# Matmul with RMSNorm: the right half of row blocks 2 and 3 as seven Strassen products, streamed with B

## The chip, the cores and the metric

The kernel runs on one core of a Trainium2 chip. The metric is the device time of one execution in microseconds (us); the median of three runs of the kernel before is 224.25 us (224.13 to 224.69).

## The reference

```python
# a: 2048x2048, b: 2048x2048, gamma: 2048, all fp32; eps = 1e-5
x = np.matmul(a, b)
rms = np.sqrt(np.mean(x ** 2, axis=-1, keepdims=True) + eps)
return gamma * x / rms
```

So each row of the product is divided by its own root mean square and multiplied by gamma. A row can be written out only when all of its 2048 columns are known.

## The kernel before

**Tiles.** A is cut into 16 row blocks of 128 rows, B into eight pieces of 256 rows (`KP`, each piece two steps `kt` of 128), and each of these into a left and a right half of 1024 columns (`j` = 0, 1; one half has two chunks of `CH` = 512 columns). B is cast to bf16 while it is loaded and stays on the chip. A matmul has 128 rows of A, 128 of k and 512 columns, and writes one PSUM bank. There are eight banks: seven in the pool `ps_a` (tiles `acc`), handed out in the order in which they come free, and one in `ps_t` (`tbank`).

**Head.** Row blocks 0 to 3 (`HB` = 4) are computed the plain way while B arrives. In the left half (loop over `kp`, `groups1`) TensorE transposes each arriving piece of A (`transpose_head`, L160), VectorE copies it into `head_at`, and seven chunks collect in seven banks; the eighth (row block 3, chunk 1) goes through `tbank` in parts that VectorE adds up (`stream_in_parts`, L379). In the right half (`groups2`) it is the same with seven chunks in seven banks and no transposes of the head; the eighth chunk follows at the end by itself (L459 to L466).

**Body.** Row blocks 4 to 15 are taken in pairs, the groups `g` = 2 to 7. Such a group has 256 rows; with a half of B it makes a 2x2 block product, computed by Strassen's scheme in seven products of 8 matmuls instead of eight. `a_sums` (L238) builds the sums of A's quarters (`s_sum`, 128x1024 16-bit each), `b_sums` (L249) three sums of B's quarters per piece into `sums`, and `b_sum_7`, `b_sum_6` and `b_sums_in_place` put two more in place of B's own quarters, which may happen only when no plain matmul needs them any more. `group_half` (L483) gives the order of products, 2, 5, 1, 4, 3, 7, 6, with these lines at its start:

```python
t = x22
at_hook(0)
product(g, j, 2, p2)
c = spare if (g, j) == (G0, 0) else t
nc.scalar.copy(out=c, in_=p2)
at_hook(1)
product(g, j, 5, p5)
nc.vector.tensor_tensor(out=t, in0=p5, in1=c, op=ALU.add)
```

Product 4 then accumulates onto the bank of product 2, product 3 onto that of product 5 (`start=False`), so each has to wait until the earlier contents have been read.

**Rows of A for the body.** `load_block` brings 128 rows (1 MB) through GpSimd's DMA queue into one of two buffers of `a_pool`. `row_norm` (L204, ScalarE: two squares over 1024 elements with a sum, one root), `row_factor` (L215, four short steps on VectorE) and `row_apply` (L226, VectorE for blocks 4 and 5, ScalarE after that) scale the rows to fp16. Blocks 4 and 5 are transposed by TensorE (`transpose_half`, L174, copied out by VectorE), the others by DMA (`transpose_dma`, on SP's queue).

**End of a row.** `square` (L287, ScalarE) sums the squares of 512 columns; `take_rms` (L313) adds them up on VectorE and takes the root on ScalarE; `finish` (L334) multiplies by gamma and 1/rms on VectorE, half a row at a time, and issues the output DMA from SP. The eight half-row buffers `x_slot` are used again: row block 4's left half takes the place of row block 0's left one, row block 5's left half (where the first group's `x21`, `x22` lie) that of row block 0's right one.

**What sets the order.** The schedule is written by hand (`manual_schedule`): every engine works strictly in the order in which the program calls it, and waits are put in where data or a buffer demands it. The `hooks` of `hooks_of` (L535) place side work between the products. GpSimd's queue of loads is written out as a list, `later` (L357): pieces 0 to 4 of B's right half, row block 4, B 5, B 6, row block 5, B 7; then gamma, blocks 6 and 7 (these wait until blocks 4 and 5 have left `a_pool`), and later blocks after a `wait_for`.

Of the kernel before, what the change touches and what calls it, by code (L numbers as in the profile page):

```python
# [17 lines left out]
def kernel(  # L18
# [32 lines left out]
    stat_pool = ctx.enter_context(tc.tile_pool(name="stat_pool", bufs=8))  # L51
# [25 lines left out]
    spare = head_at.rearrange("p t r m -> p (t r m)")[:, K:2 * K].bitcast(FP32)[:, 0:CH]  # L77

    def a16_slot(mb):

        if mb < HB + 2:
            return x_slot[HB + 1 + 2 * (mb % 2)].bitcast(FP16)
        flat = head_at.rearrange("p t r m -> p (t r m)").bitcast(FP16)
        return flat[:, (2 + mb % 2) * K:(3 + mb % 2) * K]
# [27 lines left out]

    def load_block(mb):
        a32[mb] = a_pool.tile([P, K], FP32, name="a32")
        nc.gpsimd.dma_start(out=a32[mb], in_=a[mb * P:(mb + 1) * P, :])
# [8 lines left out]
    identity_f = consts.tile([P, P], FP32, name="identity_f")  # L124
# [4 lines left out]
    nc.vector.memset(warm, 0.0)  # L129
    identity = consts.tile([P, P], BF16, name="identity")  # L130
# [43 lines left out]
    def transpose_half(mb, g):  # L174
        bank = ps_t.tile([P, CH], FP32, name="tbank")
# [7 lines left out]
        nc.vector.tensor_copy(out=at(mb)[:, g * 8:(g + 1) * 8, :], in_=view)  # L183
# [8 lines left out]
    def new_msq(mb):  # L192
        msq[mb] = stat_pool.tile([P, NCH + 1], FP32, name="msq")
        n_sq[mb] = 0

    for mb in range(HB):
        new_msq(mb)
        nc.gpsimd.memset(msq[mb][:, NCH:], float(eps))
# [27 lines left out]
    def row_apply(mb):  # L226
        a16[mb] = a16_slot(mb)
        if mb < HB + 2:
            nc.vector.tensor_scalar_mul(out=a16[mb], in0=a32.pop(mb), scalar1=factor.pop(mb))
# [5 lines left out]
    def quarter(g, r, c):  # L235
        return at(2 * g + r)[:, c::2, :]

    def a_sums(g, which):  # L238
# [3 lines left out]
        for s in which:  # L242
            x, y, op = terms[s]
            nc.vector.tensor_tensor(out=s_sum[s], in0=x, in1=y, op=op)  # L244
# [11 lines left out]
    def b_sum_7(j, kp):  # L256

        b21, b22 = (b_quarter(j, kp, 1, c) for c in range(2))
        nc.vector.tensor_tensor(out=b21, in0=b21, in1=b22, op=ALU.add)

    def b_sum_6(j, kp):

        b11, b12 = (b_quarter(j, kp, 0, c) for c in range(2))
        nc.vector.tensor_tensor(out=b12, in0=b12, in1=b11, op=ALU.add)

# [6 lines left out]
    def product(g, j, m, bank, start=True):  # L272
        for kp in range(KP):
            lhsT = {3: quarter(g, 0, 0), 4: quarter(g, 1, 1)}[m] if m in (3, 4) else s_sum[m]
            rhs = {1: lambda: sums[j][:, 0, kp, :], 2: lambda: b_quarter(j, kp, 0, 0),
                   3: lambda: sums[j][:, 1, kp, :], 4: lambda: sums[j][:, 2, kp, :],
                   5: lambda: b_quarter(j, kp, 1, 1), 6: lambda: b_quarter(j, kp, 0, 1),
                   7: lambda: b_quarter(j, kp, 1, 0)}[m]()
            nc.tensor.matmul(bank, lhsT[:, kp, :], rhs,  # L279
                             start=(start and kp == 0), stop=(kp == KP - 1),  # L280
                             skip_group_check=not start)
# [5 lines left out]
    def square(mb, src):  # L287
# [3 lines left out]
        nc.scalar.activation(out=sq[:, 0:CH], in_=src, func=ACTF.Square,  # L291
                             scale=inv_sqrt_n, accum_out=msq[mb][:, c:c + 1])
# [60 lines left out]
    def new_bank():  # L353
        return ps_a.tile([P, CH], FP32, name="acc")

    later = ([("b", kp) for kp in range(5)]
             + [("a", HB), ("b", 5), ("b", 6), ("a", HB + 1), ("b", 7)])  # L357

    def load_later(n):
        for _ in range(min(n, len(later))):  # L360
            kind, which = later.pop(0)
            load_b(1, which) if kind == "b" else load_block(which)
# [31 lines left out]

    groups1 = [(r, c) for r in range(HB) for c in range(2)][:-1]
    last1 = (HB - 1, 1)
    banks = {}
    for r in range(HB):
        x_tile(r, 0)
    transpose_first()  # L400
    for kp in range(KP):
# [4 lines left out]
        before = [lambda: transpose_head(kp + 1)] if kp + 1 < KP else []  # L406
        stream(groups1, kp, before, len(groups1) + 5 if kp == 0 else None)
# [3 lines left out]
        if kp > 0:  # L411
            b_sums(0, kp - 1)
    load_later(2)
    b_sums(0, KP - 1)


    def prepare(mb):
        row_norm(mb)
        row_factor(mb)
        row_apply(mb)  # L420

    def b_sums_2(kp):
        b_sums_in_place(0, kp)
        b_sums(1, kp)
        if kp + 1 < KP:
            b_sum_7(1, kp)

    r3 = HB - 1
    squares = groups1 + [last1]
    groups2 = [(r, c) for r in range(HB) for c in (2, 3)][:-1]  # L430
    for kp in range(KP):
        load_later(1)
        before = [lambda: transpose_half(HB, 0)] if kp == 6 else []
        if kp == 7:
            before = [lambda: transpose_half(HB, 1)]
        stream(groups2, kp, before)
        square(squares[kp][0], x_chunk(*squares[kp]))
        if kp == 4:
            prepare(HB)
        if kp == 6:  # L440

            prepare(HB + 1)
        elif kp == KP - 1:
            b_sums_in_place(0, kp - 1)
        else:
            b_sums_2(kp)
# [3 lines left out]


    def squares2(r):
        for c in (2, 3):
            square(r, x_chunk(r, c))

    evict(groups2[0:2], ())
    squares2(0)
    evict(groups2[2:-1], ())
    bank = new_bank()  # L459
    for kt in range(KT):  # L460
        if kt in (0, 6):
# [275 lines left out]
```

## Time and profile before

| what | value |
|---|---|
| median of the runs | 224.25 us |
| span of the profiled execution, first to last instruction | 222.6 us |
| what lies between the two | 1.65 us |
| TensorE matmul busy | 211.1 us, 95% |
| VectorE busy | 161.8 us, 73% |
| ScalarE busy | 129.1 us, 58% |
| GpSimd busy | 24.5 us, 11% |
| mean granted TensorE clock | 0.993 |
| DMA moved | 47.13 MB, 212 GB/s |

The profile shows one execution. The profiled execution's own device time is not given beside its span, so the median of the runs stands for it. Times are from the start of the span; L279 is line 279 of the kernel, PEld is TensorE's loading of weights. A line of a group or of the timeline has the source line, the engine, the operation, output<-inputs and the shape. Duration is that of one instruction alone; where two follow each other on one engine, the second may start some 0.1 us before the first one's end.

### The profile page before, as it was taken

The page shows a single profiled execution, that of the slowest core. Times are in us where ns is not written, and L with a number is a line of the kernel's source. Part 1 is how long each engine was busy: PE and PEld are TensorE (multiplying, and loading weights), DVE is VectorE, ACT ScalarE, POOL GpSimd, SP SyncE. Part 2 cuts the span into 40 slices and gives each one's busy share as a digit, 9 for nine tenths or more (in the row PEclk, how much of TensorE's full clock was granted, in tenths as well). Part 3 has the DMA queues.
Part 4 walks back from the last instruction along what each step waited for, and adds up shares of the span by engine and source line. Part 5 has one row for each costly group of instructions (what it writes and reads, how often), then busy time and mean ns, then how long its engine had stood idle before and what let it go on. Part 6 is the DMA issues. An engine that isn't in the chain of part 4 may idle for free.

```text
span 222.6 us, 3026 instructions
## 1 busy us (share of the span) xinstructions
PE 211.1 (95%) x1043; PEld 98.6 (44%) x1043; DVE 161.8 (73%) x324; ACT 129.1 (58%) x272; POOL 24.5 (11%) x49
## 2 busy tenths in 40 slices
PE   7899999999999999999999999999999999999950
PEld 2445444444454444444444444444444444444430
DVE  2427557983999989978949298837994589587692
ACT  3110002807698895799646985699478954334570
POOL 7534232300000001000100002000200000000000
PEclk9999999999999999999999999999999999999997
DMA  6999999999973499818889259945994794044045
GB/s 184 223 202 209 203 208 211 212 303 259 327 280 159 188 272 292 310 72 226 276 228 400 58 174 222 366 151 143 246 368 168 97 282 189 0 188 193 0 190 188
DMA packets 36176, 47.13 MB, mean 212 GB/s; under 512 B 21952, under 2 KB 26048, under 8 KB 34496
## 3 DMA queue, kind: packets, MB, share of 16 engines
q0 software_dynamic: 9648, 23.33, 41.6%
q1 hardware_dynamic: 26080, 22.29, 33.0%
q10 hardware_dynamic: 432, 1.31, 2.0%
q8 instruction: 8, 0.13, 0.2%
q14 instruction: 8, 0.07, 0.1%
HBM read 34.60 MB, written 16.78 MB: 231 GB/s over the span
## 4 chain that ended last, share of the span: by engine, by line
PE 83%; DMA 8%; DVE 2%; POOL 2%; issue 1%; ACT 1%; DVEq 0%; ACTq 0%; POOLq 0%
PE acc L279 63%; PE acc L350 18%; DMA b<-in_b_dram 8%; POOL early L106 1%; DVE x L617 1%; POOL b L100 1%; DVE x L620 1%; PE tbank L179 1%; PE tbank L382 1%; PE tbank L165 1%; ACT sq L291 0%; DVEq L732 0%; ACT sq L682 0%; DVE x L690 0%; DVE r L322 0%
## 5 line engine op out<-in xcount | busy, mean ns | idle before, releaser
L279 PE MATMUL acc<-b,s 128*128 128x512 bf16 x376 | 83.3, 379 | 0.0
L279 PEld LDWEIGHTS <-s 128*128 128x128 f16 x472 | 46.2, 98 | 55.7 <-DVE s L244 0.2
L350 PE MATMUL acc<-b,head_at 128*128 128x512 bf16 x240 | 55.1, 379 | 0.6 <-DMA b<-in_b_dram 0.4
L291 ACT ACTIVATE sq<-x 128x512 bf16<-128x512 f32 x62 | 39.1, 631 | 10.9 <-DVE x L520 5.1
L340 DVE SCALAR_TENSOR_TENSOR x<-x,r,gamma_sb 128x1024 f32<-128x1024 f32 x28 | 34.7, 1282 | 0.8
L209 ACT ACTIVATE sq<-a 128x1024 bf16<-128x1024 f32 x24 | 25.4, 1057 | 16.8 <-DMA a<-in_a_dram 16.4
L350 PEld LDWEIGHTS <-head_at 128*128 128x128 bf16 x240 | 22.9, 98 | 26.7 <-issue 1.1
L393 ACT COPY x<-acc 128x512 f32<-128x512 f32 x11 | 5.9, 591 | 25.1 <-PE acc L350 25.1
L231 ACT ACTIVATE head_at<-a,s 128x2048 f16<-128x2048 f32 x10 | 19.9, 1990 | 0.0
L279 PEld LDWEIGHTS <-at_even 128*128 128x128 f16 x96 | 9.4, 98 | 11.5 <-issue 0.4
L279 PEld LDWEIGHTS <-head_at 128*128 128x128 f16 x96 | 9.4, 98 | 11.3
L100 POOL DMA_DIRECT2D b<-in_b_dram x15 | 10.6, 708 | 16.0 <-DMA b<-in_b_dram 13.2
L217 DVE TENSOR_SCALAR s<-norm 128x1 f32<-128x1 f32 x12 | 1.8, 150 | 14.3 <-ACT norm L212 14.2
L244 DVE TENSOR_TENSOR s<-at_even 128x1024 f16<-128x1024 f16 x15 | 9.7, 684 | 2.8 <-DMA at_even<-head_at 2.8
L291 ACT ACTIVATION_READ_ACCUMULATOR sq<-x 128x1 f32 x62 | 11.7, 188 | 0.0
L279 PE MATMUL acc<-t_left,s 128*128 128x512 bf16 x48 | 11.3, 379 | 0.0
L279 PE MATMUL acc<-early,s 128*128 128x512 bf16 x48 | 11.3, 379 | 0.0
L279 PE MATMUL acc<-early,at_even 128*128 128x512 bf16 x48 | 11.0, 379 | 0.0
L279 PE MATMUL acc<-t_left,at_even 128*128 128x512 bf16 x48 | 10.9, 379 | 0.0
L509 ACT COPY x<-acc 128x512 f32<-128x512 f32 x10 | 5.7, 575 | 8.9 <-PE acc L279 8.9
L279 PE MATMUL acc<-t_left,head_at 128*128 128x512 bf16 x48 | 10.8, 379 | 0.0
L279 PE MATMUL acc<-early,head_at 128*128 128x512 bf16 x48 | 10.8, 379 | 0.0
(86 smaller groups left out, 205.8 us busy)
## 6 DMA issues: line engine op xcount, KB each, us to landing
out_dram<-x SPq DMA_DIRECT2D x30, 512.0 KB, 3.1
a<-in_a_dram POOLq DMA_DIRECT2D x12, 1024.0 KB, 8.5
b<-in_b_dram POOLq DMA_DIRECT2D x15, 512.0 KB, 17.1
early<-in_a_dram POOLq DMA_DIRECT2D x7, 256.0 KB, 14.8
early<-in_b_dram ACTq DMA_DIRECT2D x2, 512.0 KB, 5.9
gamma_sb<-in_gamma_dram POOLq DMA_DIRECT2D x1, 1024.0 KB, 19.9
out_dram<-x SPq DMA_DIRECT2D x3, 256.0 KB, 3.5
early<-in_a_dram SPq DMA_DIRECT2D x1, 512.0 KB, 5.7
```

The costliest lines, as they stand in the source:

```text
L100: nc.gpsimd.dma_start(out=raw[j][kp], in_=b[kp * W2:(kp + 1) * W2, j * HALF:(j + 1) * HALF].rearrange("(t p) n -> p t n", p=P))
L106: nc.gpsimd.dma_start(out=ah(kp), in_=a[0:HB * P, kp * W2:(kp + 1) * W2].rearrange("(r p) k -> p r k", p=P))
L165: nc.tensor.matmul(view[:, t, r, :], ah(kp)[:, r, t * P:(t + 1) * P], identity, is_transpose=True, start=(t == 0 and r == 0), stop=(t == 1 ...
L209: nc.scalar.activation(out=junk, in_=a32[mb][:, h * HALF:(h + 1) * HALF], func=ACTF.Square, scale=2.0 ** -8, accum_out=n2[:, h:h + 1])
L231: nc.scalar.activation(out=a16[mb], in_=a32.pop(mb), func=ACTF.Copy, scale=factor.pop(mb))
L244: nc.vector.tensor_tensor(out=s_sum[s], in0=x, in1=y, op=op)
L279: nc.tensor.matmul(bank, lhsT[:, kp, :], rhs, start=(start and kp == 0), stop=(kp == KP - 1), skip_group_check=not start)
L291: nc.scalar.activation(out=sq[:, 0:CH], in_=src, func=ACTF.Square, scale=inv_sqrt_n, accum_out=msq[mb][:, c:c + 1])
L340: nc.vector.scalar_tensor_tensor(out=x, in0=x, scalar=r, in1=gamma_sb[:, h * HALF:(h + 1) * HALF], op0=ALU.mult, op1=ALU.mult)
L350: nc.tensor.matmul(bank, head_at[:, kt, r, :], head_rhs(c, kt), start=(kt == 0), stop=(kt == KT - 1))
L393: copy(out=x_chunk(*g), in_=banks[g])
L509: nc.scalar.copy(out=x21, in_=p2)
```

## The change

- Row blocks 2 and 3 (`PAIR`) keep the plain scheme in the left half. In the right half, blocks 0 and 1 stay plain (four banks, `plain`), and blocks 2 and 3 become one 2x2 block product by Strassen's seven products. Products 2, 5 and 1 are accumulated piece by piece as B arrives (`stream_right`, three banks); products 4, 3, 7 and 6 follow after the stream, with the transposes of blocks 4 and 5 between them.
- The pair's sums of A are made by VectorE from `head_at`: three of them behind the copies of the transposed head in the left half (`early_sums`), the rest in the right half. Their combination (`x11` to `x22`) takes two steps during the stream's end, and four more steps in the first group (`pair_sums`, `pair_ends`).
- B's sums in place: five pieces of the left half are summed during the left half, the right half's in one step per piece during the right half; `b_sum_7` and `b_sum_6` go.
- The loads are reordered: all eight pieces of B's right half, then row blocks 4 and 5 in halves of a row.
- `row_apply` of blocks 4 and 5 writes to `head_at` instead of to `x_slot`; block 4's transposed banks are copied out by ScalarE, block 5's by VectorE; their second banks come from `ps_a`.
- The first group (`g` = 2, left half) takes product 5 before product 2 and keeps `t` in a buffer of its own; `finish(0)` moves into it, behind product 2. Roots (`take_rms`) of rows 0 to 2 are called apart from `finish`, row 0's ahead of the norms of blocks 6 and 7. Squares of the right half take 1024 columns in one instruction (`square_half`).
- At the start ScalarE takes a root of a constant, `identity_f` lies in `t_left`, and four memsets are added on GpSimd. `msq` has a pool of its own.

```diff
+    spare = [spare[:, 0:CH], consts.tile([P, CH], FP32, name="t_first")]
     def a16_slot(mb):
-        if mb < HB + 2:
-            return x_slot[HB + 1 + 2 * (mb % 2)].bitcast(FP16)
...
+    def load_half(mb, h):
+        if h == 0:
+            a32[mb] = a_pool.tile([P, K], FP32, name="a32")
+        nc.gpsimd.dma_start(out=a32[mb][:, h * HALF:(h + 1) * HALF],
+                            in_=a[mb * P:(mb + 1) * P, h * HALF:(h + 1) * HALF])
...
+    nc.vector.memset(pace, 1.0)
+    nc.scalar.activation(out=pace, in_=pace, func=ACTF.Sqrt)
...
+        nc.gpsimd.memset(msq[mb][:, NCH - 1:NCH], 0.0)
...
+    def square_half(mb, h):
+        c = n_sq[mb]
+        n_sq[mb] += 1
+        sq = sq_pool.tile([P, 2 * CH], BF16, name="sq")
+        nc.scalar.activation(out=sq, in_=x_tile(mb, h), func=ACTF.Square,
+                             scale=inv_sqrt_n, accum_out=msq[mb][:, c:c + 1])
...
-    later = ([("b", kp) for kp in range(5)]
-             + [("a", HB), ("b", 5), ("b", 6), ("a", HB + 1), ("b", 7)])
+    later = [("b", kp) for kp in range(KP)] + [("a", n) for n in range(4)]
...
+    early_sums = {4: ((2,), 0, 6), 5: ((5,), 0, 7), 6: ((1,), 0, KP)}
...
+        if kp in early_sums:
+            before.append(lambda: a_sums(PAIR, *early_sums[kp]))
...
+        if 0 < kp < KP - 2:
+            b_sums_in_place(0, kp - 1)
...
+    def stream_right(kp):
+        order = [(g, kt) for kt in (2 * kp, 2 * kp + 1) for g in plain]
+        if kp in (0, KP - 1):
+            order.sort(key=lambda x: plain.index(x[0]))
+        if kp == KP - 1:
+            for m in (2, 5):
+                pair_matmul(m, kp)
+            pair_matmul(1, kp - 1)
+        for g, kt in order:
+            if kt == 0:
+                banks[g] = new_bank()
+            head_matmul(banks[g], *g, kt)
+        if kp < KP - 1:
+            for m in (2, 5):
+                pair_matmul(m, kp)
+            if kp > 0:
+                pair_matmul(1, kp - 1)
+        else:
+            pair_matmul(1, kp)
     for kp in range(KP):
         load_later(1)
+        b_sums(1, kp)
+        stream_right(kp)
         square(squares[kp][0], x_chunk(*squares[kp]))
+        if kp > 0:
+            b_sums_in_place(1, kp - 1)
+        if kp == 0:
+            b_sums(0, KP - 1)
+            b_sums_in_place(0, KP - 3)
+        if kp == 1:
+            b_sums_in_place(0, KP - 2)
+            b_sums_in_place(0, KP - 1)
+        if kp == 2:
+            a_sums(PAIR, (2,), 6, KP)
+            a_sums(PAIR, (5,), 7, KP)
+        if kp in (3, 4):
+            a_sums(PAIR, ((7, 6)[kp - 3],))
...
+    nc.scalar.copy(out=x22, in_=pair[2])
+    nc.vector.tensor_tensor(out=x22, in0=pair[5], in1=x22, op=ALU.add)
+    evict(plain, (2, 3))
+    b_sums_in_place(1, KP - 1)
+    product(PAIR, 1, 4, pair[2], start=False)
+    row_norm(HB)
+    row_norm(HB + 1)
+    nc.vector.tensor_tensor(out=x22, in0=pair[1], in1=x22, op=ALU.subtract)
+    row_factor(HB)
+    product(PAIR, 1, 3, pair[5], start=False)
+    row_apply(HB)
+    nc.scalar.copy(out=x21, in_=pair[2])
+    row_factor(HB + 1)
+    row_apply(HB + 1)
...
+    product(PAIR, 1, 7, p7, within={5: [lambda: turn(HB, 0)]})
+    turn(HB, 1)
+    for g in range(2):
+        take_transposed(HB, g, turned[HB, g], nc.scalar.copy)
+    nc.scalar.copy(out=x12, in_=pair[5])
+    p6 = new_bank()
+    product(PAIR, 1, 6, p6)
+    a_sums(G0, (5,))
+    for g in range(2):
+        turn(HB + 1, g)
+        take_transposed(HB + 1, g, turned[HB + 1, g], nc.vector.tensor_copy)
+    square_half(0, 1)
+    def pair_sums():
+        a_sums(G0, (2, 1))
+        take_rms(0)
+        nc.vector.tensor_tensor(out=x11, in0=x22, in1=x21, op=ALU.add)
+        nc.vector.tensor_tensor(out=x22, in0=x22, in1=x12, op=ALU.add)
+    def pair_ends():
+        nc.vector.tensor_tensor(out=x11, in0=p7, in1=x11, op=ALU.add)
+        nc.vector.tensor_tensor(out=x22, in0=p6, in1=x22, op=ALU.add)
...
-        t = x22
+        first = (g, j) == (G0, 0)
+        c, t = spare if first else (x22, x22)
         at_hook(0)
         p2, p5 = new_bank(), new_bank()
-        product(g, j, 2, p2)
-        c = spare if (g, j) == (G0, 0) else t
-        nc.scalar.copy(out=c, in_=p2)
+        one, two = ((5, p5), (2, p2)) if first else ((2, p2), (5, p5))
+        product(g, j, *one)
+        nc.scalar.copy(out=c, in_=one[1])
         last_squares()
         at_hook(1)
-        product(g, j, 5, p5)
-        nc.vector.tensor_tensor(out=t, in0=p5, in1=c, op=ALU.add)
+        product(g, j, *two)
+        nc.vector.tensor_tensor(out=t, in0=two[1], in1=c, op=ALU.add)
...
+                hook(0, pair_sums)
+                hook(1, square_half, 1, 1)
+                hook(1, row_norm, nxt)
                 hook(1, row_norm, nxt + 1)
                 hook(2, a_sums, g, (7, 6))
+                hook(2, take_rms, 1)
+                hook(2, finish, 0, (1, 0))
+                hook(2, row_factor, nxt)
+                hook(2, apply, nxt)
+                hook(2, pair_ends)
+                hook(3, square_half, r2, 1)
+                hook(3, finish, 1)
+                hook(3, row_factor, nxt + 1)
+                hook(5, apply, nxt + 1)
+                hook(5, square_half, r3, 1)
+                hook(7, take_rms, r2)
...
-                hook(1, squares2, r3)
-                for kp in range(KP):
-                    hook(2, b_sum_6, 1, kp)
+                hook(2, finish, r2)
```

## The prediction

> **What bounds the kernel now.** I read the page first, then the chain that ended last, then the timelines of ScalarE, VectorE and GpSimd from 30 to 100 us, then stretches of engine time.
>
> The page's first part (busy us and share) and two pieces of the chain (start, us, what):
>
> ```profile
> PE 211.1 (95%) x1043; PEld 98.6 (44%) x1043; DVE 161.8 (73%) x324; ACT 129.1 (58%) x272; POOL 24.5 (11%) x49
> ```
> ```profile
> 7.18 17.47 DMA b<-in_b_dram
> ...
> 40.00 19.64 PE acc L350 x91
> ...
> 69.41 140.08 PE acc L279 x648
> ```
>
> Until 24.64 us the chain waits for B; from there TensorE never pauses until 209.5. A matmul of 512 columns costs 140.08/648 = 0.216 us. So a matmul taken out is worth 0.216 us, as long as nothing else becomes late. The next question is who is nearly late. Stretches of engine time (columns: stretch, sum, then PE, PEld, DVE, ACT, POOL busy):
>
> ```profile
> 62.00:70.00 8.00, 8.00 (x57) 4.38 (x55) 7.40 (x17) 7.34 (x16) 0.53 (x1) 1.00 0.67 260
> 70.00:78.00 8.00, 8.00 (x39) 3.58 (x37) 7.49 (x21) 6.91 (x13) 0.00 (x0) 1.00 0.33 133
> 78.00:86.00 8.00, 8.00 (x39) 3.64 (x38) 7.11 (x12) 6.51 (x14) 0.00 (x0) 1.00 0.94 247
> ```
>
> From 62 to 86 us VectorE and ScalarE are some 90% busy: what is added there can turn into a wait of TensorE. GpSimd's timeline (start and length of the issue) and, for the same stretch, the DMA issues (last column: us to landing) show the other near limit:
>
> ```profile
> 41.37 0.70 POOL L100 DMA_DIRECT2D b<-in_b_dram  x1 [1.93 <-DMA b<-in_b_dram]
> ```
> ```profile
> b<-in_b_dram POOLq DMA_DIRECT2D x1, 512.0 KB, 20.0
> ```
>
> The last piece of B's right half lands at 41.37 + 20.0 = 61.4. TensorE starts the right half at 40.0 and wants that piece seven rounds of 14 matmuls (3.02) and one set of transposes (0.45) later, at 61.6. The same sum for the earlier ones gives landings at 38.6, 41.1, 43.6, 46.1, 48.6 (B's pieces 0 to 4), 51.1 (block 4), 53.6, 56.0 (B 5, 6), 58.5 (block 5): one MB read each 2.48 us, from one queue.
>
> **What the Trainium skill says.** "ScalarE: Activation LUTs", section "What ACT_TABLE_LOAD costs": about 1283 ns for a load of tables, and 186 ns + 0.833 ns per element for an ACTIVATE with immediates. The trace agrees: 1283 ns, and 1057 ns for 1024 elements (formula 1039). "VectorE: DVE Perf Modes", section "The perf-mode tier table": tensor_tensor runs at double rate on 16-bit SBUF data and at the plain rate on fp32 or PSUM. The trace agrees: 684 ns for 1024 16-bit elements and for 512 fp32 ones. "DMA: Bandwidth & Descriptors", section "Anatomy of one DMA": about 2.0 us + bytes/436e3. The 2.48 us pitch fits the second term (2.40); block 7, alone in its queue, took 6.6 us against 4.4 by the formula, so I use 6.6.
>
> **The change, part by part.** Back to back, a step takes 0.60 us on VectorE (its row says 0.68, the ends overlap), 1.20 for a scale by gamma; on ScalarE 0.47 for a copy from PSUM, 0.75 for a square of 512, 1.18 for one of 1024, 2.58 for a norm (two squares and a root), 1.90 for an apply of 2048, 0.11 for a root alone.
>
> TensorE: the right half of blocks 2 and 3 was 4 chunks x 16 = 64 matmuls and becomes 7 products x 8 = 56. **Minus 8 x 0.216 = 1.73 us.** All else on TensorE keeps its count.
>
> Left half. VectorE gets five in-place sums (0.60) and three sums of A (0.47, 0.53, 0.60) in rounds of 3.9 us that hold 0.6 + 0.6 + 1.0 so far. Copying the transposed head starts 0.3 us late at worst, and TensorE wants the bank 1.5 us after it asks. Cost 0. The four small memsets on GpSimd (0.2 us) stand ahead of loads that then queue for 10 us: 0. The early root moves a table load (1.28 us) from 53.55 into ScalarE's idle start: off the path now.
>
> Right half. TensorE starts at 40.0 as before and runs 64 + 24 = 88 matmuls, so it wants B's piece k at 42.2 + 2.38 (k - 1): 51.7, 54.1, 56.4 for 5 to 7. With both blocks behind B, these land in the slots 51.1, 53.6, 56.0. Slack 0.4 to 0.6, hence no stall on paper; b7 once took 2.83 instead of 2.48, so I book 0 and keep 0.7 (piece 5 on, three pitches of 0.35 more, less the 0.4) as the upper end. The halves of blocks 4 and 5 have no row: taken at half the pitch, 1.24 each, no less, and up to 1.5; ScalarE wants block 4's second half at 59.9, so neither end costs anything. VectorE has for each round b_sums 1.0 and an in-place sum 0.6, plus what is left of A's sums (1.5) and three in-place sums of the left half: from 41.65 it is busy to 58.2, each first sum ready before TensorE asks for it. A's sums read bf16 with a stride; nearest row, with the same stride in fp16, 684 ns (0.60). At the page's plain rate they would take some 1.2: then VectorE is 1.2 late at the end of the stream and block 4's apply costs TensorE 1.0. No gain is possible below 0.60, since the rate is already the double one. I take 0.60 and keep the other end among what I don't see.
>
> Turn to the groups. TensorE ends the stream at 59.0; products 4, 3 and five matmuls of 7 bring it to 63.5, where block 4 must be scaled. Block 4 lands at 58.5; ScalarE has copied x22 and two chunks by 58.7, norms to 61.3 and 63.9. VectorE: x22, two evictions, the in-place sum and x22 again fill 58.2 to 61.2; factor 0.7, apply 1.28: 63.35. Met, by 0.2. ScalarE then copies x21, takes block 4's two transposed banks (no row; the 1057 ns row and the page's 1039 say 1.0; taken 1.0 each; at VectorE's 0.6 ScalarE only idles longer before the root below, at 1.4 the first group starts 0.1 later: 0 to 0.1) to 66.3, x12, a square: 67.9. The sum for product 5 is ready at 67.0. TensorE: 7's rest, 6 and the four transposes (0.45) end at 67.7, not 69.4. Then VectorE's two copies, sums 2 and 1 (69.4: product 2 waits 0.05) and the reduction for row 0's root end at 70.15.
>
> First group, left half: **here I find the new wait.** ScalarE stood idle from 67.9 to 70.15 for that root, and has now in order: root 0.11, copy of p5 0.47, half square 1.18, norms of blocks 6 and 7 5.16, root 0.11, apply 1.90, half square 1.05, x21 with its square 1.23, x12 with its square 1.23, apply 1.90, half square 1.05, root 0.11, and then the right half's copy of p2, 0.55. Sum 16.05: **86.2**. (Before, block 6's norm was done by 69.4, ahead of the group.) Product 4 of the right half accumulates on the bank that this copy reads; behind it stands TensorE's whole queue. TensorE is there at 67.75 + 10 x 1.727 = 85.0. **Plus 1.2 us.** Before, the copy ran at 84.26, the product at 86.7:
>
> ```profile
> 84.26 0.59 ACT L498 COPY x<-acc 128x512 f32<-128x512 f32 x1
> ```
>
> Checks beside it: VectorE has pair_sums, t 72.05 (product 4 at 72.9 reads its bank: met thanks to t's own buffer, since row 0's output leaves only at 74.8), sums 73.2, finish(0) 75.9, factor 76.6, pair_ends 77.8 (bank wanted at 79.8), p1 78.4, finish(1) 81.0, factor 81.7 (ScalarE's second apply at 82.6): no longer wait. Moving finish(0) behind the group start costs 0, since x21's copy comes at 80.2 and row 0's bytes left by 78. SP sees the same outputs and transposes in order. Blocks 6 and 7: issued 0.57 us after the applies (63.9, 66.5), landing after 6.6 at 70.5 and 73.1; wanted at 71.9 and 74.5. The second group starts at 93.2 with its sums at 90.7; from there all runs as before.
>
> Sum: -1.73 + 0.05 + 1.2 + 0.1 (half of a short stall by B) = **-0.4 us**. The profiled span is 222.6; its own time is not given apart, and 1.65 us lie between it and the median 224.25. 222.6 - 0.4 + 1.65 = **223.85**.
>
> **The rivals.**
> 1. *Full gain.* ScalarE reaches the p2 copy by 85.0, if its 16.05 us are 1.2 less. For: before, it idled 3 us in 77 to 87. Against: the sum of rows. Time 224.25 - 1.7 = 222.55.
> 2. *B bounds the right half.* The pitch slips to 2.83 in pieces 5 to 7; 0.7 us more, and blocks 4 and 5 as late. For: slack of 0.4 and one such landing. Against: eight at 2.48. 223.85 + 0.7 = 224.55.
> 3. *Block 7 is late: slower.* ScalarE's in-order norm stands before everything in the first group. Each us after 74.5 at which block 7 lands is a us of stall. For: block 6 took 8.5 us behind another transfer. Against: 6.6 alone. If it takes 10 (76.5), 2.0 more: 225.85. It turns slower than before by more than 0.67 when block 7 lands after 75.6.
>
> **How the numbers follow.** 0.3% (0.67 us) is about what a measurement of this kernel can tell from no change. Forecast 0.47, its own range 223.3 to 224.5 (ScalarE's sum 0.5 off either way); rival 1 0.23; rival 2 0.13; rival 3 0.12; 0.05 for a stall that I don't see, also slower. Faster by 0.67 or more (under 223.58): rival 1 and a quarter of the forecast, 0.35. Slower (over 224.92): rival 3, the unseen, a third of rival 2: 0.21. Same: 0.44. Range 222.5 to 225.2: forecast, rivals 1 and 2.
>
> **What would show it.** In the profile after: 1035 instead of 1043 PE matmuls; no PE wait for B after 40 us (or rival 2); the first group's start near 67.7; one PE pause of about 1.2 us near 85 ended by ScalarE's copy of the right half's p2 (absent: rival 1; ScalarE waiting on block 7 before it: rival 3). Wrong altogether if TensorE pauses at block 4's transposes, near 63.5, by more than 0.3 us, or if the pause at 85 is ended by VectorE.

## The result and the profile after

The changed kernel takes **232.75 us** (median of 4 runs, 231.20 to 233.99) against 224.25 before: a ratio of 1.037, 95% interval 1.033 to 1.042. The forecast was 223.85 us, with a range of 222.5 to 225.2. The profiled execution took 233.99 us, its span is 232.2, so 1.8 us lie outside it (before: 1.65). The spans differ by 9.6 us.

First the page's busy time (us and share of the span):

```profile
PE 212.0 (91%) x1015; PEld 98.3 (42%) x1035; DVE 168.4 (72%) x330; ACT 127.8 (55%) x263; POOL 25.7 (11%) x55
```

The weight loads fell from 1043 to 1035: the eight matmuls are gone (20 more matmul records are merely missing). Yet PE was busy 0.9 us longer (in part through the eleven warm-up matmuls at the start, 4.87 against 3.92 us, which hold nothing up) and its share fell by four points, so it stood idle, and was slower somewhere. TensorE's timeline shows where. The bracket is the idle time ahead of a row and what ended it:

```profile
67.55 3.73 PE L289 MATMUL acc<-b,s 128*128 128x512 bf16 x15
...
83.20 1.89 PE L289 MATMUL acc<-early,s 128*128 128x512 bf16 x8
86.65 3.61 PE L289 MATMUL acc<-early,at_even 128*128 128x512 bf16 x16 [1.56 <-ACT x L566]
90.10 3.62 PE L289 MATMUL acc<-b,s 128*128 128x512 bf16 x15
100.90 5.89 PE L289 MATMUL acc<-b,s 128*128 128x512 bf16 x16 [7.18 <-DVE s L264]
```

Up to 83 us TensorE runs as forecast: the first group starts at 67.55, before at 69.25 in the same view, 1.70 us earlier. (The forecast's 67.7 counts from the chain's 69.41 for that start, 0.16 later.) Then there are two pauses. The one at 85 is the forecast's, ended by ScalarE's copy of product 2. The one of 7.18 us at 94 is not in the prediction at all, and the 16 matmuls after it take 5.89 us instead of 3.62. Rows that follow each other without a pause overlap by 0.16 us (before, a row of 1.89 us starts at 84.84 and the next one 1.73 later, at 86.57), so a pause costs its idle time and 0.16. That gives the whole account of the two profiled executions: -1.70 (the group starts earlier: the eight matmuls) + 1.72 + 7.34 + 2.28 (5.89 less the normal 3.61) = **+9.6**, measured +9.6.

The chain that ended last says what the long pause waits for (start, length, what):

```profile
82.47 1.90 ACT head_at L246
...
84.39 15.73 DMA head_at<-head_at
...
100.15 0.70 DVE s L264
...
100.90 11.29 PE acc L289 x41
```

The DMA `head_at<-head_at` is the transpose of row block 7, issued the moment ScalarE has scaled it. It takes 15.7 us. The rows of SP, VectorE and GpSimd beside it, of the kernel after:

```profile
84.39 1.91 SPq L199 DMA_TRANSPOSE head_at<-head_at  x1
```
```profile
83.62 0.68 DVE L593 TENSOR_TENSOR x<-acc,t_first 128x512 f32<-128x512 f32 x1
```
```profile
84.37 0.19 POOL L126 COPY pace<-x 128x1 f32<-128x1 f32 x1 [17.59 <-DVE tot L339]
84.89 1.05 POOL L120 DMA_DIRECT2D a<-in_a_dram  x2 [0.34 <-issue]
```

and of the kernel before:

```profile
82.89 1.71 SPq L186 DMA_TRANSPOSE head_at<-head_at  x1
```
```profile
87.12 0.68 DVE L525 TENSOR_TENSOR x<-acc,x 128x512 f32<-128x512 f32 x1
```
```profile
87.87 0.18 POOL L121 COPY pace<-x 128x1 f32<-128x1 f32 x1 [22.86 <-DVE x L525]
88.37 1.06 POOL L115 DMA_DIRECT2D a<-in_a_dram  x2 [0.32 <-issue]
```

Before, the loads of blocks 8 and 9 came 5.5 us after the transpose was issued. After, they come 0.5 us after it: VectorE finishes the first group's last sum, `x22` (L593, before L525), at 84.30 instead of 87.80, 3.5 us earlier, and this is what `wait_for` in `load_after` waits for. (The bracket of GpSimd's row names `tot`, VectorE's next instruction; that one doesn't write the chunk that GpSimd copies.) The DMA issues of that stretch, last column the median us to landing, before (76 to 90 us) and after (78 to 102 us):

```profile
out_dram<-x SPq DMA_DIRECT2D x4, 512.0 KB, 3.4
a<-in_a_dram POOLq DMA_DIRECT2D x2, 1024.0 KB, 6.9
head_at<-head_at SPq DMA_TRANSPOSE x2, 4.3
```
```profile
out_dram<-x SPq DMA_DIRECT2D x4, 512.0 KB, 9.2
a<-in_a_dram POOLq DMA_DIRECT2D x2, 1024.0 KB, 16.2
head_at<-head_at SPq DMA_TRANSPOSE x2, 10.1
```

The loads became more than twice as slow. The other two lines are medians that mix: of the two transposes after, block 6's took 4.4 us and block 7's 15.7, and of the four outputs, row 1's two took some 3.7 us and row 2's two, in the collision, 14.6 (before, 3.7). Stretches of engine time of the kernel after (columns as in the prediction; the last three are granted clock, DMA share, GB/s):

```profile
86.00:94.00 8.00, 7.01 (x31) 3.03 (x31) 3.84 (x5) 4.55 (x11) 0.00 (x0) 1.00 1.31 104
94.00:100.00 6.00, 0.00 (x0) 0.00 (x0) 0.00 (x0) 0.41 (x1) 0.00 (x0) 0.89 0.72 254
100.00:104.00 4.00, 3.10 (x8) 1.16 (x9) 3.75 (x7) 2.19 (x5) 0.00 (x0) 0.50 0.77 315
104.00:108.00 4.00, 4.00 (x17) 1.60 (x16) 3.39 (x12) 3.27 (x6) 0.00 (x0) 0.81 0.01 2
```

From 86 to 94 the DMA engines are full (busy share 1.31) but move 104 GB/s. (In e8 below, with the same loads and four outputs but no transpose in this stretch, they moved 323 at a share of 0.99.) From 100 on TensorE's clock is at 0.50, which is the slow 16 matmuls. "TensorE: Matmul & The Clock Gate", section "What's actually happening", says so: after an idle window of some 3.4 us the clock falls to half until TensorE has been busy as long. This trace agrees: after the pause of 7.18 us the clock is at 0.50, by 106 us it is at 1.00 again, and the pause of 1.56 us at 85 left it at 1.00.

### The profile page after: what moved, and what is told of

Its sections match the earlier page's. It is cut to its first block, busy times and chain, and to the rows that moved or that the text cites. A ratio compares the mean times of both kernels' runs of the same rounds, so it can differ in the third digit from the quotient of the medians.

```text
span 232.2 us, 2991 instructions
## 1 busy us (share of the span) xinstructions
PE 212.0 (91%) x1015; PEld 98.3 (42%) x1035; DVE 168.4 (72%) x330; ACT 127.8 (55%) x263; POOL 25.7 (11%) x55
## 3 DMA queue, kind: packets, MB, share of 16 engines
q10 hardware_dynamic: 432, 1.31, 2.0%
## 4 chain that ended last, share of the span: by engine, by line
PE 69%; DMA 14%; ACT 6%; DVE 4%; POOL 2%; issue 2%; DVEq 0%; ACTq 0%; POOLq 0%
PE acc L289 56%; PE acc L373 11%; DMA b<-in_b_dram 7%; DMA head_at<-head_at 7%; ACT sq L223 2%; POOL early L105 1%; DVE x L689 1%; ACT head_at L246 1%; ACT sq L314 1%; ACT sq L307 1%; POOL b L99 1%; DVE x L692 1%; PE tbank L404 1%; DVE s L264 1%; PE tbank L172 1%
## 5 line engine op out<-in xcount | busy, mean ns | idle before, releaser
L289 PE MATMUL acc<-b,s 128*128 128x512 bf16 x397 | 94.0, 386 | 7.8 <-DVE s L264 7.2
L289 PEld LDWEIGHTS <-s 128*128 128x128 f16 (+1 forms) x512 | 50.3, 99 | 69.1 <-DVE s L264 8.1
L373 PE MATMUL acc<-b,head_at 128*128 128x512 bf16 x171 | 41.3, 379 | 0.7 <-DMA b<-in_b_dram 0.3
L307 ACT ACTIVATE sq<-x 128x512 bf16<-128x512 f32 x54 | 34.1, 631 | 5.5 <-DVE x L689 3.0
L373 PEld LDWEIGHTS <-head_at 128*128 128x128 bf16 x176 | 16.8, 98 | 20.1 <-issue 1.2
L264 DVE TENSOR_TENSOR s<-head_at 128x1024 f16<-128x1024 f16 (+5 forms) x22 | 13.4, 638 | 9.7 <-DMA head_at<-head_at 9.6
L415 ACT COPY x<-acc 128x512 f32<-128x512 f32 x6 | 3.4, 588 | 25.0 <-PE acc L373 25.0
L289 PEld LDWEIGHTS <-head_at 128*128 128x128 f16 (+1 forms) x112 | 11.0, 98 | 13.2
L289 PE MATMUL acc<-early,head_at 128*128 128x512 bf16 x63 | 14.4, 379 | 0.1
L577 ACT COPY x<-acc 128x512 f32<-128x512 f32 x10 | 5.8, 576 | 13.1 <-PE acc L289 13.1
L99 POOL DMA_DIRECT2D b<-in_b_dram x15 | 10.6, 706 | 15.4 <-DMA b<-in_b_dram 12.8
L280 DVE TENSOR_TENSOR b<-b 128x1024 bf16<-128x1024 bf16 x16 | 10.9, 691 | 0.2
L566 ACT COPY x<-acc 128x512 f32<-128x512 f32 x9 | 5.3, 587 | 10.3 <-PE acc L289 7.3
```

Source lines behind the costliest of these rows:

```text
L99: nc.gpsimd.dma_start(out=raw[j][kp], in_=b[kp * W2:(kp + 1) * W2, j * HALF:(j + 1) * HALF].rearrange("(t p) n -> p t n", p=P))
L264: nc.vector.tensor_tensor(out=sum_of(g, s)[:, lo:hi, :], in0=x[:, lo:hi, :], in1=y[:, lo:hi, :], op=op)
L280: nc.vector.tensor_tensor(out=flat[:, 1:3, :], in0=flat[:, 1:3, :], in1=flat[:, 0::3, :], op=ALU.add)
L289: nc.tensor.matmul(bank, lhsT[:, kp, :], rhs, start=(start and kp == 0), stop=(kp == KP - 1), skip_group_check=not start)
L373: nc.tensor.matmul(bank, head_at[:, kt, r, :], head_rhs(c, kt), start=(kt == 0), stop=(kt == KT - 1))
L415: copy(out=x_chunk(*g), in_=banks[g])
```

## The experiments

Theory A: the early loads slow the transpose down, and this is the loss but for some 2 us. Rival B: the new order of work on ScalarE and VectorE is the loss (block 7's late scaling, full engines, buffers). "Rivals" inside an expectation are those of that run. Each ratio is to runs of the kernel before taken beside it (medians 224.2 to 224.5). In the cuts of code, `...` stands for lines left out.

**e1, e2, e3: when the loads start.** e1 and e3 are the kernel after with later loads; e2 is the kernel *before* with earlier ones.

```diff
 e1 (after)
-        wait_for(x_chunk(2 * g + 1, 1)[:, 0:1])
+        wait_for(at(2 * g + 3)[:, 0, 0:1] if g == G0 else x_chunk(2 * g + 1, 1)[:, 0:1])
 e2 (before)
-        wait_for(x_chunk(2 * g + 1, 1)[:, 0:1])
+        wait_for(a16[2 * g + 3][:, 0:1] if g == G0 else x_chunk(2 * g + 1, 1)[:, 0:1])
 e3 (after)
-        wait_for(x_chunk(2 * g + 1, 1)[:, 0:1])
+        wait_for(x_chunk(2 * g + 1, 3 if g == G0 else 1)[:, 0:1])
...
-                hook(0, load_after, g, nxt + 2)
-                hook(0, load_block, nxt + 3)
+                hook(1 if g == G0 else 0, load_after, g, nxt + 2)
+                hook(1 if g == G0 else 0, load_block, nxt + 3)
```

> The changed kernel, but the loads of row blocks 8 and 9 are released only when block 7's DMA transpose has landed (GpSimd waits on the transposed block). Theory A (the loads, released at 84.2 us by an earlier x22, run into the transpose issued at 84.4 and hold it for 15.7 us): the transpose lands in some 4.3 us at 88.7, the second group starts at about 93.7 with no wait of TensorE, the 7.2 us and the slow clock after them vanish; the 1.6 us wait near 85 stays. Time 223.5 to 224.5. Theory B (the transpose is slow because row 1's outputs stand before it on SP's queue): nothing of this moves, the transpose still takes over 10 us, time 231 or more.

> The kernel before, with one edit: the loads of blocks 8 and 9 are released by block 7's scaled rows, that is 0.5 us after its DMA transpose is issued (82.9) instead of 5.5 us. Theory A: this alone makes the kernel before slow: the transpose takes about 15 us, lands near 98, the second group starts at 99 instead of 93.6, and the slow clock after the pause adds 2: 230 to 233. Theory B or any theory that needs the Strassen pair: same as before, 224.2 within 0.5.

> The changed kernel, but the loads of blocks 8 and 9 are released by the right half's copy of p2, some 2.8 us after block 7's transpose is issued instead of 0.5. Theory A, with the kernel before as a measure (offsets of 2.0, 2.8 and 3.2 us gave transposes of 8.0, 7.2 and 5.8 us): the transpose takes about 7 us, lands at 91.5, sums ready at 92.2, just in time for 93.7: time 223.5 to 224.5, as with the loads held back altogether. If any overlap brings the collapse: transpose over 10 us and 228 or more.

Measured: e1 227.7 us (ratio to before 1.015, 1.013 to 1.017), e3 227.5 (1.015, 1.013 to 1.017), e2 231.7 (227.9 to 233.3, so its ratio has no useful interval; but even the lowest of its four runs is 3.6 us over before). In e1 and e3 the transpose takes 4.4 us, and the long pause and the slow clock are gone. For e3 this is better than expected: with the loads 2.8 us after it, it was to take about 7. Row 1's outputs stand ahead of it on SP's queue in all of these runs, so they aren't what makes it slow. The kernel before, with nothing changed but the date of two loads, shows the same picture as the changed one (TensorE's timeline of e2, of an execution of 231.7 us; its clock is at 0.51 from 99 to 103 us):

```profile
99.02 5.55 PE L279 MATMUL acc<-b,s 128*128 128x512 bf16 x16 [5.38 <-DVE s L244]
```

Its transpose took 15.5 us. So the collision is shown, by taking it away and by making it alone. Its size isn't what A said: e1 and e3 take away 5.0 and 5.2 us of the 8.5 (medians) and stay 3.5 and 3.3 us over before, where 223.5 to 224.5 us were expected. The account above put 9.6 us on the long pause and its clock; with it gone, pauses come to light that TensorE's delay had covered. TensorE's and ScalarE's timelines of e3 show what remains:

```profile
86.65 3.61 PE L289 MATMUL acc<-early,at_even 128*128 128x512 bf16 x16 [1.59 <-ACT x L566]
...
100.45 1.89 PE L289 MATMUL acc<-t_left,head_at 128*128 128x512 bf16 x8 [1.56 <-ACT x L566]
```
```profile
99.81 0.59 ACT L566 COPY x<-acc 128x512 f32<-128x512 f32 x1 [4.38 <-DMA out_dram<-x]
```

A second copy of a product 2, that of the next group, waits until row block 2's output has left its buffer. The output, issued behind the loads, took 9.5 us.

**e6: one load or two.** Block 9's load is held until the transpose has landed, block 8's stays beside it.

```diff
+                if g == G0:
+                    hook(0, lambda: wait_for(at(nxt + 1)[:, 0, 0:1]))
                 hook(0, load_block, nxt + 3)
```

> The changed kernel, but of the two loads that start 0.5 us after block 7's transpose only block 8's stays there; block 9's waits until the transpose has landed. If the hold grows with the bytes loaded beside it: the transpose takes about 10 us instead of 15.7, second group near 96, some 228. If one load beside it is as bad as two: 15 us, 231 to 234.

A single run: 231.4 us, within the changed kernel's own 231.2 to 234.0, so the time tells nothing. The trace does: the transpose took 12.8 us (two loads: 15.7, held back: 4.4), the one load 12.1. Here a single megabyte does most of the harm to the transpose.

**e4, e5, e7: the pauses that remain.** e4 scales block 7 earlier, before ScalarE's and VectorE's work on rows 1 and 2, moves row 3's square into the right half, and puts the sums of `(G0, 1)`, the first group's right half, into the `t` of its left half; e5 moves row 2's root and the first group's squares as well and uses that `t` in the next group's left half too; e7 is e3 with the buffer alone, for both.

```diff
 e4 and e5
+                hook(3, row_factor, nxt + 1)
+                hook(3, apply, nxt + 1)
                 hook(3, square_half, r2, 1)
                 hook(3, finish, 1)
-                hook(3, row_factor, nxt + 1)
-                hook(5, apply, nxt + 1)
-                hook(5, square_half, r3, 1)
...
+                hook(1, square_half, r3, 1)
 e7 (e5 too)
-        c, t = spare if first else (x22, x22)
+        own = g == G0 or (g, j) == (G0 + 1, 0)
+        c, t = spare if first else (spare[1],) * 2 if own else (x22, x22)
```

> The changed kernel with the wait rule of its loads untouched, but block 7's factor and apply come directly behind block 6's (transpose issued near 81 instead of 84.4), the square of row block 3's right half behind the right half's copy of p2, and that copy goes to t's own buffer. Theory A: the loads now start some 4 us after the transpose, which lands near 85.5: no long wait; and the copy of p2 comes at 85.2 instead of 86.6, so that the 1.6 us wait near 85 shrinks to 0.2. Time 222.2 to 223.0, faster than both. Theory B: the transpose is still long, over 10 us, but from 81: second group at about 96, 226 or more.

> The changed kernel with everything that the traces so far name: block 7's factor and apply directly behind block 6's (its transpose ends before the loads of 8 and 9 start), the first group's two squares on ScalarE, the square of row block 3's right half and the root of row block 2 behind the right half's copy of p2, and that copy and the next group's first copy in t's own buffer, so that they wait for no output DMA. If the four waits found are all of it: TensorE's pause near 85 and the one near 100 are gone, the second group starts at 92.0, and 1.6 of the 1.73 us of the eight matmuls remain: 222.5 to 223.0, faster than both kernels. If something else costs: 224 or more.

> Loads of blocks 8 and 9 held back as in e3_loads_mid, and only the buffers changed: the right half's copy of p2 in the first group and the first copy of the next group go to t's own buffer instead of to half-rows whose output may still be on its way. If the waits near 85 and 100 are for outputs: the one at 100 goes (1.6 + 0.16 of pipeline), the one at 85 shrinks from 1.6 to 1.0 (ScalarE's own queue ends at 85.4), block 9's norm comes earlier and the third group's wait goes too: 224.7 to 225.4 against 227.5. If they are ScalarE's queue alone: 227.5 as before.

Measured: e4 227.2 us (1.013, 1.011 to 1.014), e5 226.1 (1.008, 1.007 to 1.010), e7 **237.0** (1.057, 1.053 to 1.061). All three miss what was expected of them. In e4 and e5 the transpose is undisturbed (4.7 us) and the pauses shrink, but they move more than they go: e5 has 0.77 us at 86 (the copy waits for `t`, which VectorE still reads), 1.01 at 94 (VectorE's `finish` of row 2 waits 3.46 us for a root that stands behind five squares on ScalarE), 0.15, 0.60 and 0.27 later. e7 is my own repetition of the mistake under study. GpSimd's timeline:

```profile
81.07 0.18 POOL L126 COPY pace<-x 128x1 f32<-128x1 f32 x1 [14.30 <-DVE s L231]
81.59 0.53 POOL L120 DMA_DIRECT2D a<-in_a_dram  x1 [0.34 <-ACT sq L307]
84.64 0.53 POOL L120 DMA_DIRECT2D a<-in_a_dram  x1 [2.52 <-ACT head_at L246]
```

With the copy of product 2 in another buffer, nothing new is written to the chunk that releases the loads. The wait ends with the last write to the same space, VectorE's `finish` of row 1 at 81.0, so the loads start at 81.6 and 84.6 instead of 87.2, on both sides of the transpose at 84.4. That one takes 19 us, and TensorE waits 11.1. The pause near 86 did shrink as expected (1.59 to 0.92).

**e8, e9: a buffer that is really free.** e8 is e5 with the sums of `(G0, 1)` in the space of the scaled block 6, which has been transposed by then; row 2's root comes at hook 5 and its right half leaves first; the next group's copy goes back to `x22`. The cut shows what differs from the kernel after and isn't in e5. e9 also holds every pair of loads until the odd block's transpose has landed.

```diff
 e8
+    t_second = head_at.rearrange("p t r m -> p (t r m)")[:, 2 * K:2 * K + 2 * CH].bitcast(FP32)
-        c, t = spare if first else (x22, x22)
+        own = (g, j) == (G0, 1)
+        c, t = spare if first else (t_second,) * 2 if own else (x22, x22)
...
-                hook(7, take_rms, r2)
+                hook(5, take_rms, r2)
...
-                hook(2, finish, r2)
+                hook(2, finish, r2, (1, 0))
 e9 (e8 and)
-        wait_for(x_chunk(2 * g + 1, 1)[:, 0:1])
+        wait_for(at(2 * g + 3)[:, 0, 0:1])
```

> Block 7 is scaled and transposed before the loads of blocks 8 and 9 are released; the sums of the right half of row blocks 4 and 5 collect in a buffer of their own (free space of the scaled block 6), so that the copy of product 2 waits neither for an output nor for the first group's t; row 2's root comes early, so that its squares hold nobody up. Theory (the loss is the transpose in the loads' way, and what remains are waits for buffers and roots, each removable): TensorE's pauses near 86 and 94 to 100 fall from 0.8 and 1.0 us (the kernel with all steps moved) to some 0.2 each, those near 120 (0.6) and 127 (0.3) stay: 224.3 to 225.0 us. Rival (ScalarE and VectorE have simply no room left in this group, so that any order leaves about two us of pauses): the pauses come back elsewhere, 226 or more.

> As the kernel with the second buffer, and the loads of two blocks ahead are held until the odd block's transpose has landed, in every group. Theory: block 9's transpose takes 4 to 5 us instead of 8, the pause near 120 (0.6 us) goes, and no later block is late, as each has some 20 us to spare: 223.7 to 224.4 us. Rival (loads are needed as early as they come now): the norms of blocks 10 and later wait, and the time is 225 or more.

Measured: e8 **224.7 us**, ratio 1.0014 (0.9996 to 1.0032): as expected, and no difference from before. The whole loss is undone, so what the collision left of it was of rival B's kind: order and buffers. From 25 to 97 us TensorE does not pause. After that (its timeline):

```profile
97.62 1.89 PE L290 MATMUL acc<-t_left,head_at 128*128 128x512 bf16 x8 [0.37 <-ACT x L568]
99.80 1.89 PE L290 MATMUL acc<-t_left,head_at 128*128 128x512 bf16 x8 [0.29 <-DVE x L572]
...
117.76 3.63 PE L290 MATMUL acc<-b,s 128*128 128x512 bf16 x16 [0.54 <-DVE s L265]
```

0.37 + 0.29 + 0.54 and three times 0.16 make 1.68 us: Strassen's 1.73, given back. e9 took 231.2 us (1.028, 1.024 to 1.031), as its rival had it. Block 9's transpose did shorten, from 8.1 to 5.1 us, and its pause went. But in the profiled execution (228.9 us, the fastest of the six) the loads of blocks 10 and 11 come 3.0 us later, and in each later group ScalarE's norm, which stands ahead of the copy of product 2, waits for them (pauses of 1.57, 1.65 and 1.01 us). In this kernel those loads may come neither beside a transpose nor three microseconds later.

**e10, e11, e12: who takes the last 1.7 us.** e11 is e8 with block 9 scaled and transposed ahead of row 4's outputs. e10 has that too and moves block 8's norm, and with it its factor and scaling and block 9's norm, behind the copy of product 2. e12 is e11 with row blocks 1 and 2 computed but never written out.

```diff
 e11
-                hook(4 if g == G0 + 1 else 3, finish, 2 * g - 2)
+                if g > G0 + 1:
+                    hook(3, finish, 2 * g - 2)
                 hook(4, apply, nxt + 1)
+                if g == G0 + 1:
+                    hook(4, finish, 2 * g - 2)
 e10 (this and)
+                    hook(8, row_norm, nxt)
...
-                hook(0, row_factor, nxt)
+                hook(2 if second else 0, row_factor, nxt)
 e12 (e11 and)
+            if mb not in (1, 2):
                 nc.sync.dma_start(out=rows(mb, h * HALF, (h + 1) * HALF), in_=x)
```

> As the kernel with the second buffer; in the second group block 8's norm stands behind the copy of product 2 on ScalarE, block 8's factor behind the sum t on VectorE, and block 9 is scaled and transposed before row block 4's outputs are issued. Theory (the gain of Strassen is there until 97 us, and three pauses of 0.37, 0.29 and 0.54 us take it back, each with 0.16 us of lost overlap): all three go, the time falls by 1.5 to 1.7 us against the kernel with the second buffer (224.7), to 223.0 to 223.2 us, under both given kernels. Rival (block 9 waits for its load and nothing else, and later norms come late as well): the pauses stay in size and only change place, 224.2 to 225 us.

> As the kernel with the second buffer, with one edit: block 9 is scaled and transposed before row block 4's outputs are issued, so that its transpose is issued near 106.8 instead of 108.9 us and the loads of blocks 10 and 11 start 4 us after it instead of 2. Theory: the transpose takes 4.5 to 5.5 us instead of 8.1, the pause of 0.54 us at 117.8 goes, and with it 0.7 us: 224.0 us. Rival (the transpose is slow for another reason than the loads): no change, 224.7 us.

> As the kernel with block 9's transpose first, but row blocks 1 and 2 are computed and never written out (2 MB less of output, issued from 83.8 to 88.9 us). Theory (what takes the last of the gain back is that block 8 lands at 93.9 us whenever TensorE is done, because its load from 86.0 shares the DMA with these four outputs): the load takes 5.5 to 6 us instead of 8, block 8's norm is done by some 94.3 instead of 96.7, the pauses of 0.29 and 0.44 us at 99 and 122 go, and the time is 222.7 to 223.3 us. Rival (VectorE and ScalarE are too full there, whatever the loads do): at most 0.3 us faster than the 224.6 of the kernel with the outputs.

e10: 227.3 us (1.013, 1.011 to 1.015), a miss: the copy waits until 97.2 for an output to leave its buffer, and the norm, now behind it, starts at 97.7 (in e8, where it stands ahead of the copy, it started at 94.1, when its block had landed). ScalarE's timeline of e10:

```profile
97.19 0.59 ACT L568 COPY x<-acc 128x512 f32<-128x512 f32 x1 [6.04 <-DMA out_dram<-x]
```

e11: 224.6 us (1.0009, 0.9996 to 1.0022). Transposed block 9 lands after 4.3 instead of 8.1 us and the pause of 0.54 is gone, as expected. The loads are not the whole reason, as the edit also takes the transpose away from the outputs issued right before it: in e9, behind the same outputs and with the loads far off, it took 5.1. The time did not follow: a pause of 0.44 appears at 122, ended by the copy behind block 10's norm, whose load is late. One reason why the gain never gets further is seen in ScalarE's timelines of before and of e11:

```profile
93.92 1.06 ACT L209 ACTIVATE sq<-a 128x1024 bf16<-128x1024 f32 x1 [1.33 <-DMA a<-in_a_dram]
```
```profile
94.03 1.06 ACT L224 ACTIVATE sq<-a 128x1024 bf16<-128x1024 f32 x1 [2.62 <-DMA a<-in_a_dram]
```

Block 8 lands at the same moment, although TensorE is 1.6 us ahead and the loads are issued 2.4 us earlier (86.0 against 88.4). The DMA issues of 84 to 100 us tell why, e11 first and e12 below it:

```profile
out_dram<-x SPq DMA_DIRECT2D x4, 512.0 KB, 6.5
a<-in_a_dram POOLq DMA_DIRECT2D x2, 1024.0 KB, 10.1
```
```profile
a<-in_a_dram POOLq DMA_DIRECT2D x2, 1024.0 KB, 6.2
out_dram<-x SPq DMA_DIRECT2D x1, 512.0 KB, 3.7
```

In e11 four outputs of half a megabyte share the DMA with the two loads; in before only two outputs and a transpose preceded them, and the loads had a median of 6.9 us. Without rows 1 and 2 the loads take 6.2, ScalarE starts block 8's norm at 91.2 without waiting for the load, TensorE does not pause after 25 us, and e12 takes **222.9 us**, ratio 0.9935 (0.9921 to 0.9948), as expected. That is 1.5 of the 1.73 us, for a kernel that leaves 2 MB of its output out. It takes two limits away at once: the traffic beside the loads, and the hold of row 2's output on the buffer that the second group's copy of product 2 writes, which in e10 lasted until 97.2. In e12 that copy runs at 93.8. The runs don't separate the two.

## Why the prediction was wrong, point by point

- *Eight matmuls, 1.73 us*: right; the first group starts 1.70 us earlier, and in e12 1.5 us come through to the end of the span.
- *Left half 0, no stall by B, the early table load*: right. TensorE has no notable wait between 24.66 and 85 us, and the right half starts at 39.98. In the profile of e4 the last B piece cost a wait of 0.5 us at 56.9, so the slack was thin, as rival 2 had it. (TensorE's date for that piece is 56.5 by the prediction's own formula, not 56.4.)
- *Turn to the groups*: right. ScalarE's copies of block 4's banks took 1.01 us (taken: 1.0, without a row to show it), and the first group started when forecast.
- *ScalarE's list of 16.05 us ends at 86.2, TensorE waits 1.2*: right in mechanism, mis-sized. The root came at 70.02, ScalarE was through at 85.4, 0.25 earlier than the sum; then the copy waited 0.52 us more, for row 1's output to leave the same buffer (`[0.52 <-DMA out_dram<-x]` at 86.01). The cost was 1.72, not 1.2. The term lacked the buffer's other reader and the lost overlap of 0.16. (With another buffer, in e7, the pause was 0.92.)
- *"SP sees the same outputs and transposes in order", "from there all runs as before"*: **this is the step that failed.** The order on SP was indeed unchanged. But what became earlier was the release of GpSimd's loads: I moved `x22` forward and did not ask what waits for it. `load_after`, 0.5 us behind block 7's transpose, was the answer. The transpose took 15.7 us instead of the 4.3 that it took before, and the second group, said to start at 93.2 with its sums ready at 90.7, got them at 100.85 and started at 100.9. In the profiled execution that is 7.34 + 2.28 us of idle time and slow clock; taking the collision away gave 5.0 to 5.2 us back (e1, e3). The rest of the 8.5 are ScalarE's list and the waits of the next groups, which "all runs as before" also put at nothing.
- *Moving finish(0) costs 0*: no run charges it. Row 0's outputs are issued at 74.8 instead of 72.2 us, far from the loads. The four outputs next to the loads in e8 and e11 are those of rows 1 and 2.
- *Rival 3, block 7 late*: right in its victim, wrong in its cause, place and price; that it said "slower" is luck. Block 7's load was not late (ScalarE goes into its norm at 74.34 without idling); its transpose was. And the clock added 2.3 us to a pause of 7.2, which the rival's price left out.
- The trace of before held the warning. Its own transpose of block 9, issued 2.0 us ahead of two loads, took 8.0 us, while that of block 7, which had 5.5 us for itself, took 4.3 (the DMA issues at 107 to 110 and at 82.5 to 83.5 us). I used the second number and never looked at the first. (Not all of the difference is the loads': block 9's transpose also stands directly behind outputs, which alone makes it 5.1.)

What stays open: by which mechanism a load slows a transpose so much (both are on the same 16 DMA engines, as "DMA: Bandwidth & Descriptors", section "Issuing engines are not separate DMA queues", says of all queues; that explains sharing, but not that the sum falls to 104 GB/s); and how the last 1.7 us divide between the traffic and the buffer. Dividing the load into smaller pieces wasn't tried, nor was e11 with the second group's copy in another buffer.

## What to carry to other kernels

For every step that a change makes *earlier*, list who waits for it, GpSimd's and SP's DMA issues above all, and what is in flight at the new date; here an earlier release cost more than the eight matmuls brought. Look in the trace of before for the same DMA at its worst neighbour, not at its best or its median. And when the pauses are cured and the time still doesn't fall, ask what date does not move with the engine that became faster: here the landing of the next row block, and the output that still held the next buffer.

## What the runs showed of the hardware

- A DMA transpose of 128 x 2048 fp16 values takes 4.2 to 4.7 us where no load comes near and no output is issued right before it (only block 14's took 4.5 to 6.0, for which no cause was sought). With two loads of 1 MB issued 0.3 to 0.5 us after it, it took 15.5 to 15.7 us; with one such load 12.8 (one run); with one on each side 19.
- The later the loads, the less. Behind outputs issued right before it (0.1 us): 7.6 to 8.4 us with loads 2.0 us after it, 6.8 to 7.7 at 2.8, 5.7 to 6.1 at 3.2, 5.1 (once 5.7) when none came within 5.7 us. Clear of outputs: 4.4 at 2.8 (e3), 4.3 at 4.1 (e11).
- The loads suffer too: 16.2 us beside the transpose and outputs, 10.1 beside four outputs (e8, e11), 6.9 in before (medians of two). Row 2's outputs took 14.6 us in the collision, 9.6 to 10.6 next to the loads without a transpose (e8), 3.7 in before.
- Pauses of TensorE up to 1.65 us left its clock at full speed; after 4.3 to 11.1 us, 16 matmuls took 5.6 to 6.2 us instead of 3.6.
